# A log-sum-exp kernel: the bias of three heads added on GpSimd, most tiles loaded whole, and the last batch written in four parts

## The chip, the cores and the metric

One core of one Trainium2 chip runs the kernel. The metric is the device time of one execution in microseconds (us). The kernel before took 341.03 us, the median of 11 runs (340.31 to 341.71). The profile shows one execution that took 341.08 us by the same clock; its span, from the first to the last instruction, is 339.1 us.

## The reference

```python
B, S, D, H = 8, 2048, 2048, 8            # x: (B, S, D) f32, bias: (H, D // H) f32
x_heads = x.reshape(B, S, H, Dh).transpose(0, 2, 1, 3) + bias[None, :, None, :]
x_tiled = np.repeat(x_heads, 2, axis=2)  # every row twice
mx = x_tiled.max(axis=-1, keepdims=True)
lse = mx.squeeze(-1) + np.log(np.exp(x_tiled - mx).sum(axis=-1))   # (B, H, 2 S)
```

For each batch, row and head, 256 values get that head's bias; the logarithm of the sum of their exponentials is written twice side by side. The input has 134.2 MB, the output 1.05 MB.

## The kernel before

**Tiles.** A tile `xt` holds 256 rows of one batch: 128 partitions with K = 2 rows of 2048 numbers, 2 MB. There are 64 tiles, 8 to a batch, and NBUF = 9 buffers for them. The kernel takes no maximum; it sums exp(x + bias), and the eight heads are split by how the bias comes in.

**Heads 0 and 1 (NPE = 2).** `add_bias` (L139 to L151) makes x + bias in PSUM on TensorE. For each of the two rows k it first writes the bias with a small bf16 matmul (L145), then adds x by a matmul with the identity (L150; each f32 matmul appears as two instructions). ScalarE takes the exponential in PSUM and sums it in the same instruction (`sum_biased`, L156), whose sum is fetched by a following read of the accumulator.

**Heads 2 to 7.** ScalarE replaces x by exp(x) in the tile (`exp_inplace`, L164), for a whole tile in one instruction of 3072 numbers a partition. VectorE multiplies each head's 256 values by exp(bias), held in `w_rep` in SBUF, and sums them (`weigh`, L170): 12 instructions a tile, each with a read of the accumulator.

**Results.** Sums of a batch are collected in `R[b]` (of the last batch only the first seven tiles; the last tile has `Rz`). `finish` (L181) transposes them on TensorE (L186), takes the logarithm and doubles it on ScalarE (L199) and stores it (L214). A full batch is finished two tiles after its end, with one transfer of 64 rows of 2 KB. The last batch is finished in three parts: the seven tiles (eight transfers of 7 rows, one a head) after the first piece of the last tile's second row, and the two rows of the last tile at the very end, one transfer each, all on SyncE's queue.

**Order.** The order of each engine's instructions is that of the program (`manual_schedule`). SyncE issues all loads. `load(t + 9)` (L248) stands after the work of tile t, since it reuses that tile's buffer. A transfer on SyncE's queue also waits for the one eight transfers earlier: eight semaphores are used in turn, which the trace shows in the semaphores that the issues name. `pieces` (L68) sets how a tile is loaded and worked on: tiles 0 to 54 whole; 55 to 59 in two rows of 1 MB; 60 to 62 in four halves of 512 KB; the last tile, 63, in seven pieces (`LAST_CUTS`, L22), down to 128 KB.

GpSimd works only at the start: it splits the bias in three bf16 parts (L116 to L120) and moves them with three small transfers of its own (L122).

Of the kernel before, what the change touches and what calls it, by code (L numbers as in the profile page):

```python
# [9 lines left out]
F32 = mybir.dt.float32  # L10
BF16 = mybir.dt.bfloat16
ACT = mybir.ActivationFunctionType
ALU = mybir.AluOpType


K = 2


NPE = 2
NBUF = 9  # L20

LAST_CUTS = [[0, 1024, 2048], [0, 512, 1024, 1536, 1792, 2048]]  # L22
# [3 lines left out]
def kernel(  # L26
# [6 lines left out]
    nc = tc.nc  # L33
    P = nc.NUM_PARTITIONS
    B, S, D = x.shape
    H, Dh = bias.shape
    assert D == H * Dh and S % (P * K) == 0
    NBLK = S // (P * K)
    T = B * NBLK
    CPE = NPE * Dh  # L40
    CW = D - CPE
    MM = 512
    assert CPE <= MM

    sb = ctx.enter_context(tc.tile_pool(name="sb", bufs=1))
    pp = ctx.enter_context(
        tc.tile_pool(name="pp", bufs=1, space=bass.MemoryType.PSUM)
    )

    brow = sb.tile([1, D], F32, name="brow")  # L50
    w_rep = sb.tile([P, CW], F32, name="w_rep")
    ident = sb.tile([P, P], F32, name="ident")
    ones = sb.tile([1, P], F32, name="ones")
    ones3 = sb.tile([3, P], BF16, name="ones3")
# [1 line left out]
    bparts = sb.tile([1, 3, CPE], BF16, name="bparts")  # L56
    brest = sb.tile([1, 2, CPE], F32, name="brest")

    nblk = [NBLK] * (B - 1) + [NBLK - 1]
    R = [sb.tile([P, K, H, nblk[b]], F32, name=f"R{b}") for b in range(B)]  # L60
    Rz = sb.tile([P, K, H], F32, name="Rz")
    junk = [sb.tile([P, Dh], F32, name=f"junk{i}") for i in range(2)]
    res = [sb.tile([H * NBLK, P, K, 2], F32, name=f"res{i}") for i in range(2)]
    xts = [sb.tile([P, K, D], F32, name=f"xt{i}") for i in range(NBUF)]
    ps = [pp.tile([P, MM], F32, name=f"ps{i}") for i in range(6)]
    tps = [pp.tile([P, K, P], F32, name=f"tps{i}") for i in range(2)]

    def pieces(t):  # L68

        left = T - 1 - t  # L70
        if left > 8:
            return [(0, K, 0, D)]
        if left > 3:
            return [(k, k + 1, 0, D) for k in range(K)]
        cuts = [[0, D // 2, D]] * K if left else LAST_CUTS
        return [
            (k, k + 1, c0, c1) for k in range(K) for c0, c1 in zip(cuts[k], cuts[k][1:])
        ]

    def rows_of(t):  # L80

        b, blk = divmod(t, NBLK)
        v = x[b, blk * P * K : (blk + 1) * P * K, :]
        if t < T - 1:
            return v.rearrange("(p k) d -> p k d", k=K)
        return v.rearrange("(k p) d -> p k d", k=K)

    def load(t):
        for k0, k1, c0, c1 in pieces(t):
            nc.sync.dma_start(  # L90
                out=xts[t % NBUF][:, k0:k1, c0:c1], in_=rows_of(t)[:, k0:k1, c0:c1]
            )
# [5 lines left out]
    for set_idx, (_name, funcs) in enumerate(get_activation_tables(nc.m.arch).items()):  # L98
        if ACT.Exp in funcs and ACT.Ln in funcs:
            nc.scalar.add_instruction(  # L100
                mybir.InstLoadActFuncSet(
                    name=nc.get_next_instruction_name(),
# [4 lines left out]
    nc.scalar.dma_start(out=brow, in_=bias.rearrange("h j -> (h j)").unsqueeze(0))  # L107
    for t in range(NBUF):
        load(t)
# [12 lines left out]
        nc.gpsimd.dma_start(out=b3[i : i + 1, :], in_=bparts[:, i])  # L122


    for i, c in enumerate(range(0, CW, MM)):
        nc.tensor.matmul(  # L126
            ps[i],
            lhsT=ones,
            rhs=brow[:, CPE + c : CPE + c + MM],
            start=True,  # L130
            stop=True,
        )
        nc.scalar.activation(out=w_rep[:, c : c + MM], in_=ps[i], func=ACT.Exp)  # L133


    n_ps = [0]
# [2 lines left out]
    def add_bias(views):  # L139

        got = []
        for v in views:
            p = ps[n_ps[0] % len(ps)]
            n_ps[0] += 1
            nc.tensor.matmul(  # L145
                p[:, 0:CPE], lhsT=ones3, rhs=b3, start=True, stop=False
            )
            got.append(p)
        for p, v in zip(got, views):
            nc.tensor.matmul(p[:, 0:CPE], lhsT=ident, rhs=v, start=False, stop=True)  # L150
        return got  # L151

    def sum_biased(p, dst):
        for h in range(NPE):
            c = h * Dh
            nc.scalar.activation(  # L156
                out=p[:, c : c + Dh],
                in_=p[:, c : c + Dh],
                func=ACT.Exp,
                accum_out=dst(h),  # L160
            )

    def exp_inplace(v):
        nc.scalar.activation(out=v, in_=v, func=ACT.Exp)  # L164

    def weigh(v, h, dst):
        c = h * Dh - CPE
        j = junk[n_junk[0] % 2]
        n_junk[0] += 1
        nc.vector.tensor_tensor_reduce(  # L170
            out=j,
            in0=v,
            in1=w_rep[:, c : c + Dh],
            scale=1.0,
            scalar=0.0,
            op0=ALU.mult,
            op1=ALU.add,
            accum_out=dst,
        )

    def finish(b, src, n_blk, k_rows, base, i, engines):  # L181

        nr = H * n_blk
        n = P * k_rows * 2
        for k in range(k_rows):
            nc.tensor.transpose(out=tps[i][0:nr, k], in_=src(k), identity=ident)  # L186
        tp = tps[i]
        rs = res[i]
        tv = bass.AP(
            tensor=tp.tensor,  # L190
            offset=tp.offset,
            ap=[[tp.ap[0][0], nr], [1, P], [P, k_rows], [0, 2]],
        )
        rv = bass.AP(
            tensor=rs.tensor,
            offset=rs.offset,
            ap=[[rs.ap[0][0], nr], [2 * k_rows, P], [2, k_rows], [1, 2]],
        )
        nc.scalar.activation(out=rv, in_=tv, func=ACT.Ln)  # L199

        parts = [(0, H)] if n_blk * n in (n, 2 * S) else [(h, h + 1) for h in range(H)]
        for q, (h0, h1) in enumerate(parts):
            rows = (h1 - h0) * n_blk
            ov = bass.AP(
                tensor=out.tensor,
                offset=out.offset + (b * H + h0) * 2 * S + 2 * base,
                ap=[[n if n_blk > 1 else 2 * S, rows], [1, n]],
            )
            iv = bass.AP(
                tensor=rs.tensor,  # L210
                offset=rs.offset + h0 * n_blk * rs.ap[0][0],
                ap=[[rs.ap[0][0], rows], [1, n]],
            )
            engines[q % len(engines)].dma_start(out=ov, in_=iv)  # L214


    for t in range(T):
        b, blk = divmod(t, NBLK)
        xt = xts[t % NBUF]
        last = t == T - 1  # L220

        def sum_at(k, h):
            return Rz[:, k, h : h + 1] if last else R[b][:, k, h, blk : blk + 1]

        for k0, k1, c0, c1 in pieces(t):
            if c0 == 0:
                got = add_bias([xt[:, k, 0:CPE] for k in range(k0, k1)])
            w0 = max(c0, CPE)
            if w0 < c1:
                exp_inplace(xt[:, k0:k1, w0:c1])  # L230
            if c0 == 0:
                for k in range(k0, k1):
                    sum_biased(got[k - k0], lambda h: sum_at(k, h))
            for k in range(k0, k1):
                for c in range(w0, c1, Dh):
                    weigh(xt[:, k, c : c + Dh], c // Dh, sum_at(k, c // Dh))
            if last and k0 == K - 1 and c0 == 0:
                finish(
                    b,
                    lambda k: R[b][:, k].rearrange("p h n -> p (h n)"),  # L240
                    NBLK - 1,
                    K,
                    0,
                    1,
                    [nc.sync],
                )
        if t + NBUF < T:
            load(t + NBUF)  # L248

        fb, at = divmod(t - 2, NBLK)  # L250
        if fb >= 0 and at == NBLK - 1:
            finish(
                fb,
                lambda k: R[fb][:, k].rearrange("p h n -> p (h n)"),
                NBLK,
                K,
                0,
                fb % 2,
                [nc.sync],
            )  # L260
    for k in range(K):
        finish(B - 1, lambda _: Rz[:, k], 1, 1, S - (K - k) * P, k, [nc.sync])

    order.__exit__(None, None, None)

# [29 lines left out]
```

The softmax here doesn't subtract the row's maximum and nothing guards it: scores larger than these inputs give would overflow.

## Time and profile before

| | |
|---|---|
| median of 11 runs | 341.03 us |
| the profiled execution, and its span | 341.08 us, 339.1 us |
| busy: ScalarE, VectorE, TensorE, GpSimd | 295.4, 271.8, 234.8, 6.3 us |
| DMA, mean over the span | 400 GB/s; 425 to 432 GB/s in the middle |
| HBM read, written | 134.23 MB, 1.05 MB |
| instructions of VectorE counted as busy | 1538 |

How to read it: rows of a page or an answer give line, engine, operation, output and inputs with their shapes, the number of instructions, their busy time and the mean of one in ns, and then the idle time just before them with what ended it. The "DMA" and "GB/s" rows cut the span into 40 equal slices of 8.48 us. The chain of waits follows the work that ended last back in time. Besides what the views print, the trace records the time of every DMA packet, and for each transfer the time at which each of the 16 DMA engines reported its share as landed; a few numbers below are read from those records and say so.

### The profile page before, as it was taken

The numbers are of one execution on the slowest core, as the hardware profiler recorded it, in microseconds if no ns is written. First come the engines' busy times: TensorE is split into PE (matmuls) and PEld (weight loads), VectorE is DVE, ScalarE is ACT, GpSimd is POOL, SyncE is SP. The second block draws the span as 40 slices with busy tenths as digits, with TensorE's granted clock in tenths as the row PEclk, the third lists the DMA queues.
The fourth block names the chain that finished last, engine by engine and source line by source line (L and its number), as shares of the span: only waits on it lengthen the run. The fifth ranks groups of instructions, "written<-read, shape, count | busy, mean of one in ns | idle before, by whom it ended". The sixth has DMA issues, their size and how long they took to land. (4 is left out here: it accounts for less than half of the span.)

```text
span 339.1 us, 3449 instructions
## 1 busy us (share of the span) xinstructions
PE 234.8 (69%) x408; PEld 67.9 (20%) x408; DVE 271.8 (80%) x1538; ACT 295.4 (87%) x609; POOL 6.3 (2%) x14
## 2 busy tenths in 40 slices
PE   6296775767785767875765775966766567887892
PEld 2032121112121111221221221321221211221220
DVE  0429999998887887897898698788798788989784
ACT  2379999998997997988998998998899899998994
POOL 6000000000000000000000000000000000000000
PEclk9999877785877785877898777598777898577655
DMA  8999999999999999999999999999999999988950
GB/s 304 429 431 426 426 431 424 431 427 426 427 426 432 425 425 429 430 427 426 431 425 425 431 429 424 430 430 425 427 426 432 430 411 420 422 349 283 308 202 17
DMA packets 12921, 135.50 MB, mean 400 GB/s; under 512 B 1625, under 2 KB 1897, under 8 KB 4577
## 3 DMA queue, kind: packets, MB, share of 16 engines
q1 hardware_dynamic: 12800, 135.27, 95.7%
q14 instruction: 20, 0.16, 0.1%
q8 instruction: 3, 0.05, 0.1%
q10 hardware_dynamic: 2, 0.01, 0.0%
q0 software_dynamic: 96, 0.00, 0.0%
HBM read 134.23 MB, written 1.05 MB: 399 GB/s over the span
## 5 line engine op out<-in xcount | busy, mean ns | idle before, releaser
L170 DVE CUSTOM_DVE_ANT_0 junk<-xt,w_rep 128x256 f32<-128x256 f32 x768 | 271.0, 420 | 63.3 <-ACT xt L164 63.0
L150 PE MATMUL ps<-xt,ident 128*128 128x512 f32 x256 | 184.0, 851 | 88.5 <-DMA xt<-in_x_dram 88.0
L164 ACT ACTIVATE xt<-xt 128x3072 f32<-128x3072 f32 (+4 forms) x83 | 179.4, 2172 | 19.3 <-DMA xt<-in_x_dram 15.0
L156 ACT ACTIVATE ps<-ps 128x256 f32<-128x256 f32 x256 | 94.6, 370 | 14.7 <-PE ps L150 9.8
L150 PEld LDWEIGHTS ps<-xt,ident 128*128 128x128 f32 x256 | 55.1, 242 | 166.6 <-DMA xt<-in_x_dram 124.6
L170 DVE DVE_READ_ACCUMULATOR2_ANT R<- 128x1 f32 x756 | 61.5, 81 | 0.0
L145 PE MATMUL ps<-b,ones 3*128 3x512 bf16 x128 | 47.2, 441 | 6.6 <-DVE R L170 6.6
L156 ACT ACTIVATION_READ_ACCUMULATOR ps<-ps 128x1 f32 x256 | 48.7, 190 | 0.0
L145 PEld LDWEIGHTS <-ones 3*128 3x128 bf16 x128 | 8.0, 96 | 82.8 <-issue 74.6
L126 PE MATMUL ps<-brow,ones 1*128 1x512 f32 x6 | 5.5, 1078 | 3.1 <-DMA brow<-in_bias_dram 3.1
L133 ACT ACTIVATE w_rep<-ps 128x512 f32<-128x512 f32 x3 | 1.8, 597 | 5.4 <-PE ps L126 5.4
L199 ACT ACTIVATE res<-tps 64x512 f32<-64x512 f32 (+2 forms) x10 | 5.3, 534 | 1.3 <-PE tps L186 1.3
L186 PEld LDWEIGHTS tps<-ident,R 128*64 128x64 f32 (+1 forms) x16 | 2.7, 171 | 9.6 <-ACT ps L156 3.6
L186 PE MATMUL tps<-ident,R 128*64 128x128 f32 (+1 forms) x16 | 4.6, 387 | 0.0
L186 PE MATMUL tps<-ident,Rz 128*8 128x128 f32 x2 | 0.8, 375 | 3.5 <-DVE Rz L170 2.8
L126 PEld LDWEIGHTS ps<-brow,ones 1*128 1x128 f32 x6 | 1.8, 324 | 5.1 <-issue 5.1
L100 ACT ACT_TABLE_LOAD x1 | 1.3, 1283 | 0.7 <-PEq L279 0.7
L122 POOL DMA_DIRECT2D b<-bparts x3 | 1.6, 540 | 0.0
L117 POOL TENSOR_TENSOR brest<-brow,bparts 1x512 f32<-1x512 f32 x1 | 1.1, 1142 | 0.1
L119 POOL TENSOR_TENSOR brest<-brest,bparts 1x512 f32<-1x512 f32 x1 | 1.1, 1142 | 0.1
L186 PEld LDWEIGHTS tps<-ident,Rz 128*8 128x8 f32 x2 | 0.2, 83 | 4.2 <-DVE Rz L170 3.1
L170 DVE DVE_READ_ACCUMULATOR2_ANT Rz<- 128x1 f32 x12 | 1.0, 82 | 0.0
(11 smaller groups left out, 3.0 us busy)
## 6 DMA issues: line engine op xcount, KB each, us to landing
xt<-in_x_dram SPq DMA_DIRECT2D x55, 2048.0 KB
xt<-in_x_dram SPq DMA_DIRECT2D x10, 1024.0 KB
xt<-in_x_dram SPq DMA_DIRECT2D x14, 512.0 KB
out_dram<-res SPq DMA_DIRECT2D x7, 128.0 KB
xt<-in_x_dram SPq DMA_DIRECT2D x3, 256.0 KB
xt<-in_x_dram SPq DMA_DIRECT2D x2, 128.0 KB
out_dram<-res SPq DMA_DIRECT2D x8, 14.0 KB
b<-bparts POOLq DMA_DIRECT2D x3, 1.0 KB, 5.8
```

What stands on the lines that cost most here:

```text
L100: nc.scalar.add_instruction(mybir.InstLoadActFuncSet(name=nc.get_next_instruction_name(), act_func_set_id=set_idx,))
L117: nc.gpsimd.tensor_sub(brest[:, 0], bp, bparts[:, 0])
L122: nc.gpsimd.dma_start(out=b3[i : i + 1, :], in_=bparts[:, i])
L126: nc.tensor.matmul(ps[i], lhsT=ones, rhs=brow[:, CPE + c : CPE + c + MM], start=True, stop=True,)
L133: nc.scalar.activation(out=w_rep[:, c : c + MM], in_=ps[i], func=ACT.Exp)
L145: nc.tensor.matmul(p[:, 0:CPE], lhsT=ones3, rhs=b3, start=True, stop=False)
L150: nc.tensor.matmul(p[:, 0:CPE], lhsT=ident, rhs=v, start=False, stop=True)
L156: nc.scalar.activation(out=p[:, c : c + Dh], in_=p[:, c : c + Dh], func=ACT.Exp, accum_out=dst(h),)
L164: nc.scalar.activation(out=v, in_=v, func=ACT.Exp)
L170: nc.vector.tensor_tensor_reduce(out=j, in0=v, in1=w_rep[:, c : c + Dh], scale=1.0, scalar=0.0, op0=ALU.mult, op1=ALU.add, accum_out=dst,)
L186: nc.tensor.transpose(out=tps[i][0:nr, k], in_=src(k), identity=ident)
L199: nc.scalar.activation(out=rv, in_=tv, func=ACT.Ln)
```

## The change

Each tile but the last two is now worked on whole. Heads 0 and 1 and the last three heads (5 to 7) are done as before. For heads 2 to 4 (NG = 3), GpSimd adds the bias to both rows of the tile in place (`g_add`, one instruction of 1536 numbers a partition), with the bias of those heads replicated in `b_rep`. One tile later, ScalarE takes the exponential of that part (`exp_inplace(g_part(t - 1))`) and VectorE sums it with one `tensor_reduce` (`g_sum`). A tile's buffer is therefore free one tile later, and the load behind it is `load(t + 8)` after tile t. `w_rep` moves from SBUF to PSUM; `ps` has four buffers for six, and both transposed outputs share one PSUM tile. The last two tiles (NLATE = 2) are done as before: tile 62 in two rows, tile 63 in the same seven pieces.

The last batch is written in four parts: its first six tiles (`R`, eight transfers of 6 rows) after the first piece of tile 63, issued by GpSimd; tile 62 (`Ry`, one transfer of 8 rows of 2 KB) after the first piece of the second row of tile 63; the first row of tile 63 before its last piece; the second row at the end; the last three on SyncE. The rows of a store are now listed in `parts`; for a full batch this is still one transfer of 64 rows.

```diff
+NG = 3
+NLATE = 2
...
-    w_rep = sb.tile([P, CW], F32, name="w_rep")
+    b_rep = sb.tile([P, NG * Dh], F32, name="b_rep")
...
-    nblk = [NBLK] * (B - 1) + [NBLK - 1]
+    nblk = [NBLK] * (B - 1) + [NBLK - 2]
+    Ry = sb.tile([P, K, H], F32, name="Ry")
...
-    ps = [pp.tile([P, MM], F32, name=f"ps{i}") for i in range(6)]
-    tps = [pp.tile([P, K, P], F32, name=f"tps{i}") for i in range(2)]
+    w_rep = pp.tile([P, CW], F32, name="w_rep")
+    ps = [pp.tile([P, MM], F32, name=f"ps{i}") for i in range(4)]
+    tpair = pp.tile([P, 2, K, P], F32, name="tpair")
+    tps = [tpair[:, i] for i in range(2)]
...
-        if left > 8:
+        if left > 1:
             return [(0, K, 0, D)]
-        if left > 3:
-            return [(k, k + 1, 0, D) for k in range(K)]
-        cuts = [[0, D // 2, D]] * K if left else LAST_CUTS
+        cuts = [[0, D]] * K if left else LAST_CUTS
...
-    for i, c in enumerate(range(0, CW, MM)):
+    for c in range(0, CW, MM):
         nc.tensor.matmul(
-            ps[i],
+            w_rep[:, c : c + MM],
...
-        nc.scalar.activation(out=w_rep[:, c : c + MM], in_=ps[i], func=ACT.Exp)
+    nc.scalar.activation(out=b_rep, in_=w_rep[:, 0 : NG * Dh], func=ACT.Copy)
+    for c in range(0, CW, MM):
+        w = w_rep[:, c : c + MM]
+        nc.scalar.activation(out=w, in_=w, func=ACT.Exp)
...
+    def g_part(t):
+        return xts[t % NBUF][:, :, CPE : CPE + NG * Dh]
+
+    def g_add(t):
+        nc.gpsimd.tensor_tensor(out=g_part(t), in0=g_part(t), in1=b_tile, op=ALU.add)
+
+    def g_sum(t):
+        b, blk = divmod(t, NBLK)
+        nc.vector.tensor_reduce(
+            out=R[b][:, :, NPE : NPE + NG, blk],
+            in_=g_part(t).rearrange("p k (h j) -> p k h j", j=Dh),
+            op=ALU.add,
+            axis=mybir.AxisListType.X,
+        )
...
+        if n_blk == 1:
+            step, parts = 2 * S, [H]
+        elif n_blk == NBLK:
+            step, parts = n, [nr]
+        else:
+            step, parts = n, [n_blk] * H
...
+        if left >= NLATE:
+
+            got = add_bias([xt[:, k, 0:CPE] for k in range(K)])
+            g_add(t)
+            w0 = CPE + NG * Dh
+            exp_inplace(xt[:, :, w0:D])
+            if t:
+                exp_inplace(g_part(t - 1))
+            for k in range(K):
+                sum_biased(got[k], lambda h: sum_at(k, h))
+            for k in range(K):
+                for c in range(w0, D, Dh):
+                    weigh(xt[:, k, c : c + Dh], c // Dh, sum_at(k, c // Dh))
+            if t:
+                g_sum(t - 1)
+        for k0, k1, c0, c1 in pieces(t) if left < NLATE else []:
+            if left == 0 and c1 == D and k0 > 0:
+
+                finish(
+                    B - 1,
+                    lambda k: Rz[:, k0 - 1],
...
-            if last and k0 == K - 1 and c0 == 0:
...
-        if t + NBUF < T:
-            load(t + NBUF)
+            if left == 0 and c0 == 0:
+                if k0 == 0:
+                    finish_batch(B - 1, nc.gpsimd)
+                elif k0 == 1:
+                    finish(B - 1, lambda k: Ry[:, k], 1, K, S - 2 * K * P, 0, nc.sync)
+        if left == NLATE:
+            exp_inplace(g_part(t))
+            g_sum(t)
+        if 0 < t and t - 1 + NBUF < T:
+            load(t - 1 + NBUF)
...
-    for k in range(K):
-        finish(B - 1, lambda _: Rz[:, k], 1, 1, S - (K - k) * P, k, [nc.sync])
+    finish(B - 1, lambda _: Rz[:, K - 1], 1, 1, S - P, 1, nc.sync)
```

## The prediction

> **What bounds the kernel now.** I read first the page (busy times, the slices, the chain), then the queue's own waits, the chain in order of time, and the groups by form for prices.
>
> ```profile
> PE 234.8 (69%) x408; PEld 67.9 (20%) x408; DVE 271.8 (80%) x1538; ACT 295.4 (87%) x609; POOL 6.3 (2%) x14
> ...
> GB/s 304 429 431 426 426 431 424 431 427 426 427 426 432 425 425 429 430 427 426 431 425 425 431 429 424 430 430 425 427 426 432 430 411 420 422 349 283 308 202 17
> ...
> q14 instruction: 20, 0.16, 0.1%
> ```
>
> No engine is full; the DMA runs flat at about 427 GB/s and falls to 280 to 350 in the last five slices. The chain, in order of time, says the same:
>
> ```profile
> 183.10 39.03 DMA xt<-in_x_dram
> ...
> 291.87 17.57 DMA xt<-in_x_dram
> ...
> 311.73 10.17 DMA xt<-in_x_dram
> ...
> 321.94 2.07 PE ps L150 x2
> ...
> 329.74 2.02 PE ps L150 x2
> ...
> 333.24 0.53 ACT xt L164
> ...
> 336.42 0.37 ACT res L199
> ```
>
> Loads until 321.9 us, then rows of tile 62 and 63 through TensorE (2.07 us a row at half clock), then ScalarE, VectorE, the transpose and the last store.
>
> Why does the rate fall? The landing records answer. Of the first load the 16 DMA engines report between 7.74 and 8.42 us, of tile 54 between 273.37 and 283.43, and at 294.27 one engine is 11.0 us behind the first, 8 behind the next slowest. That engine sets when a tile is complete. Its delay grows in steps of about 0.94 us ((11.03 - 0.68) / 11), and each step follows a packet of q14, an instruction fetch of 8 KB: the load packet behind it takes 1265 ns where others take 613. Eleven of these, before 294 us, come every 126 rows of VectorE's program (at rows 79, 205, 331 and so on; waits count as rows). So **fetching VectorE's instructions delays one of the 16 DMA engines**, and all loads wait for it. With eight transfers in flight the other 15 run ahead until the pieces shrink; then they stall, which is the fall in the slices. Their rate costs nothing; the slow engine's work does.
>
> [...]
>
> ```profile
> L170 DVE CUSTOM_DVE_ANT_0 junk<-xt,w_rep 128x256 f32<-128x256 f32 x768 | 271.0, 420 | 63.3 <-ACT xt L164 63.0
> L164 ACT ACTIVATE xt<-xt 128x3072 f32<-128x3072 f32 x55 | 151.8, 2760 | 19.3 <-DMA xt<-in_x_dram 15.0 <-DVE R L170 3.8
> L164 ACT ACTIVATE xt<-xt 128x1536 f32<-128x1536 f32 x10 | 14.7, 1474 | 0.0
> L122 POOL DMA_DIRECT2D b<-bparts x3 | 1.6, 540 | 0.0
> L117 POOL TENSOR_TENSOR brest<-brow,bparts 1x512 f32<-1x512 f32 x1 | 1.1, 1142 | 0.1
> ```
>
> **Part by part, a whole tile.** A tile's period is 4.89 us (the fast engines' 54 tiles) and about 5.0 with stores and fetches; everything that stays below it is hidden.
> - VectorE: twelve `weigh` start 0.346 us apart (timeline), 4.15 us. Now six, plus a sum of 1536. [...] 6 x 0.41 = 2.5; the sum at `weigh`'s slope (256 in 0.27) is 1.6 to 1.75. Total 4.2, hidden. Ends: 0.346 each (no loss; a gain has no reason) and 0.61 (PSUM at half rate), see rivals.
> - ScalarE: 2.67 + 1.87 = 4.54 us. Two of 1536, 1.38 apart in the timeline, cost 2.76, so 4.63, with the batch's logarithm 4.70: hidden, though with 0.3 to spare. The start (first sums at 18.2 us, unchanged, since they wait for `b3`) leaves 1.4 us more backlog, made good within some 35 tiles.
> - GpSimd: [...] it has a whole tile of slack. Ends: 1.8 us (three times the 599 ns of the one-input casts of 512 on this engine) and 5.0, where it would bind.
> - SyncE: loads go out a tile later, with six to seven tiles (over 29 us) still in flight. The slow engine never runs dry. What stands behind a waiting load on SyncE is only loads and finished batches' stores. Full batches' stores do not change. Nothing.
> - The four `ps` buffers still hold two tiles; TensorE's work is the same.
>
> **What VectorE's shorter program saves.** 24 rows a tile and 1.3 waits become 13 and one to two and a half. By tile 61 that is 870 to 950 rows: (870 - 79) / 126 = 6.3, or 6.9, so 7 fetches where there were 12. ScalarE gets one fetch more, on an engine that is only 3 us behind. Gain: 4 x 0.94 = 3.8 by 294 us and some 0.5 for the twelfth among small packets. **Larger packets:** 16 KB take 613 ns, 8 KB 312, 4 KB 159; per engine and tile 8 x 613 = 4.90, 16 x 312 = 4.99, 32 x 159 = 5.09. Five tiles save 0.09, two 0.18: 0.8 by packet times, 0.4 by landings (1.245 us a 512 KB piece). I take 0.4. Tile 61 then lands at 8.42 + 61 x 4.888 + 6 stores x 0.34 + 7 x 0.94 = 315.2, against 320.65 before; from the differences 320.65 - 4.7 = 315.9. I take **315.4**; all else follows from it (call it L).
>
> **The end: what is late next.** Loads no longer: the last piece lands at L + 10.1 = 325.5 (before 330.87). ScalarE now has, from L: tile 61, 1.38 + 1.38 (tile 60's part) + 1.87; tile 61's own part, 1.38; tile 62, two rows of 2.27 (timeline at 288 us); tile 63: 0.53 + 0.89, logarithm of R 0.5, 0.95, 0.89, logarithm of Ry 0.5, 0.53 twice, logarithm 0.3, 0.73. Sum 16.9: 332.3. GpSimd's add for tile 61, done at L + 3.5, is covered by the 4.6 before it. VectorE has two sums (1.7) and 6 + 12 + 12 `weigh`: the last sum of tile 61 ends at L + 7.8, and in order it finishes at L + 17.9 at 0.41 each. From its end to the span's end it took 339.12 - 335.95 = 3.2 us (transpose, logarithm, store). SyncE path: 315.4 + 17.9 + 3.2 = **336.5**.
>
> GpSimd's stores: the logarithm of R ends at L + 12.5 = 327.9. Eight issues of 0.54 bring the last to 331.7. Landing is the unknown. The three transfers of GpSimd in this trace took 5.8 us, but each waited twice behind 613 ns load packets; loads end at 325.5, so 4.6. [...] With 1.1 us from landing to end: 334.8 to 338.6; I take 331.7 + 4.6 + 1.1 = **337.4**. This is later than SyncE's path, so it ends the span: 339.1 - 337.4 = 1.7 saved. The profiled 341.08 stands at the median 341.03, so I predict **339.3**. The 5.2 us won in the loads shrink because ScalarE, free before the end until now, gets tile 61's extra part and the last rows all at once.
>
> **Rivals.**
> 1. TensorE takes the gain. If tile 61 finds it at half clock (as from 316.5 us on before), its rows run at 2.07 + 0.5 = 2.57 us: tile 61 until 319.7, then three rows to 327.4, transposes 1.5, the row of 63 to 331.5, where before it was 331.78. Same tail: span 338.8, 340.8 us. For: the slow rows in the chain. Against: with whole tiles the clock was full two thirds of the time.
> 2. Slower: GpSimd's stores come one by one. If each needs the 1.0 us between landings of the three small ones, and the full 5.8, the last lands at 327.9 + 7 x 1.0 + 5.8 = 340.7: span 341.8, 343.7 us. It decides from a last landing of 338.0 on (span 339.1). Against: those spacings are two load packets each.
> 3. Slower: VectorE becomes the bound. Above (5.0 - 1.75) / 6 = 0.54 us a `weigh`, each tile grows; at 0.61 it is 5.4 us, 61 x 0.4 = 24 us more, 365 us. [...] For: neither PSUM input nor overlap is in this trace. [...]
> 4. The change adds nothing to the loads, if fetches are not what delays the engine: then L stays near 320.2, and the span is about 342, 344 us.
>
> **How the numbers follow.** 0.2% (0.7 us) is about what a measurement of this kernel tells from no change. Forecast 0.62 (337.0 to 340.3); rival 1 0.14 (same); rival 2 0.10; rival 3 0.09; rival 4 0.05. Faster 0.62, same 0.14, slower 0.24. The range runs from a last store at 2 us with six fetches, which leaves SyncE's path less 1 us and VectorE at 0.346 (337.0), to 342.8, part of rival 2; left out are rival 3, most of 4, and the end of 2.
>
> **What would show it.** VectorE 856 busy instructions (2 + 62 x 13 + 2 x 24); seven of its fetches; the last engine of tile 61 about 7 us after the first; last load landed near 325.5; the slices near 427 GB/s to about 310 us; rows of `weigh` at 0.41 apart, the add at 3.4 us. Wrong, if `weigh` waits for GpSimd, if ScalarE is never idle from 60 us on, or if the loads still end near 330.

## The result, and the profile after

The changed kernel took 338.0 us, the median of 8 runs (337.75 to 338.1); the kernel before took 341.1 us in the same comparison (31 runs, 339.93 to 341.99). The ratio is 0.991, with an interval of 0.9899 to 0.9921: **0.9% faster**. The profiled execution took 338.01 us, with a span of 336.2 us, 2.9 us less than before.

These are lines of the page of the kernel after: the span, busy times, the rate of the DMA in 40 slices, the queue of instruction fetches, and two groups of transfers that GpSimd issues (last column: us from issue to landing).

```profile
span 336.2 us, 2806 instructions
...
PE 245.8 (73%) x410; PEld 71.7 (21%) x410; DVE 244.7 (73%) x856; ACT 301.4 (90%) x660; POOL 224.4 (67%) x84
...
GB/s 299 431 429 435 419 433 429 427 423 430 425 432 429 429 424 431 427 432 424 432 424 423 431 433 423 431 427 427 431 426 429 431 426 425 429 427 421 358 42 16
...
q14 instruction: 15, 0.12, 0.1%
...
out_dram<-res POOLq DMA_DIRECT2D x8, 12.0 KB, 1.7
b<-bparts POOLq DMA_DIRECT2D x3, 1.0 KB, 5.9
```

The reader sees three things. VectorE has 856 busy instructions where it had 1538, and only a tenth less busy time. The three slices before the end of the loads in which the rate fell to between 283 and 349 GB/s are gone: from the second slice it holds at 419 or more up to slice 37, which ends at 311 us. And ScalarE has gained 6 us and stands at 90% of the span.

The landing records say why the rate holds. Tile 61 was complete at 315.12 us; before, at 320.65. Its last DMA engine came 7.1 us after the first (call this the lag), where in the kernel before the lag had grown to 11.0 us by 294 us. VectorE's instruction fetches ahead of it were 7 (12 before), at its rows 70, 196, 325, 451, 577, 703 and 843. From 0.88 us of lag at the first tile (0.68 before) this is (7.11 - 0.88) / 7 = 0.89 us a fetch; the last step alone was 7.08 - 6.12 = 0.96 us.

The chain of the kernel after, in order of time (start, length, what), names loads until 319.8 us and then mostly ScalarE; the matmuls of the last rows at half clock (0.50 granted from 316.5 us on, 2.07 us a row before) are no longer in it. ScalarE's timeline shows that the loads stop deciding earlier than the chain says: from 315.21 us, 0.09 us after tile 61 landed, to 331.41 it works without a wait. What follows tile 61 until then is ScalarE's work.

```profile
285.10 32.51 DMA xt<-in_x_dram
...
317.63 2.15 DMA xt<-in_x_dram
...
319.97 2.74 ACT xt L194 x2
...
323.60 1.37 ACT xt L194
...
327.76 0.95 ACT xt L194
...
330.62 0.42 DVE junk L200
...
332.86 0.39 PE tpair L216
...
333.28 0.37 ACT res L229
```

The groups by form of the kernel after give the prices of the moved work:

```profile
L182 POOL TENSOR_TENSOR xt<-xt,b_rep 128x1536 f32<-128x1536 f32 x62 | 214.0, 3452 | 96.0 <-DMA xt<-in_x_dram 95.5 <-ACT b_rep L139 0.5
L194 ACT ACTIVATE xt<-xt 128x1536 f32<-128x1536 f32 x126 | 179.9, 1474 | 13.6 <-DMA xt<-in_x_dram 12.3
L200 DVE CUSTOM_DVE_ANT_0 junk<-xt,w_rep 128x256 f32<-128x256 f32 x396 | 140.5, 417 | 86.5 <-ACT xt L194 86.5
L186 DVE TENSOR_REDUCE R<-xt 128x6 f32<-128x1536 f32 x62 | 108.5, 1750 | 0.8 <-ACT xt L194 0.8
```

GpSimd's idle time (96.0 us) and ScalarE's idle time ahead of L194 (13.6 us) end mostly with a load: neither of them is what the tiles wait for. VectorE is idle behind ScalarE alone. A `weigh` of 417 ns is about as long as before (420).

### The profile page after: what moved, and what is told of

It is laid out like the page before. It is cut to its first block, busy times and chain, and to the rows that moved or that the text cites. A ratio compares the mean times of both kernels' runs of the same rounds, so it can differ in the third digit from the quotient of the medians.

```text
span 336.2 us, 2806 instructions
## 1 busy us (share of the span) xinstructions
PE 245.8 (73%) x410; PEld 71.7 (21%) x410; DVE 244.7 (73%) x856; ACT 301.4 (90%) x660; POOL 224.4 (67%) x84
## 4 chain that ended last, share of the span: by engine, by line
DMA 62%; ACT 22%; DVE 6%; PE 3%; issue 1%; SPq 0%; ACTq 0%; DVEq 0%
DMA xt<-in_x_dram 62%; ACT xt L194 15%; ACT ps L165 7%; DVE junk L200 4%; DVE R L186 2%; PE ps L159 2%; PE ps L154 1%; ACT res L229 1%; PE tpair L216 0%; DVE R L200 0%; DVE Rz L200 0%; SPq L95 0%; ACTq L194 0%; DVEq L356 0%
## 5 line engine op out<-in xcount | busy, mean ns | idle before, releaser
L182 POOL TENSOR_TENSOR xt<-xt,b_rep 128x1536 f32<-128x1536 f32 x62 | 214.0, 3452 | 96.0 <-DMA xt<-in_x_dram 95.5
L159 PE MATMUL ps<-xt,ident 128*128 128x512 f32 x256 | 191.3, 888 | 62.8 <-DMA xt<-in_x_dram 62.3
L200 DVE CUSTOM_DVE_ANT_0 junk<-xt,w_rep 128x256 f32<-128x256 f32 x396 | 140.5, 417 | 86.5 <-ACT xt L194 86.5
L194 ACT ACTIVATE xt<-xt 128x1536 f32<-128x1536 f32 (+1 forms) x132 | 183.4, 1435 | 13.6 <-DMA xt<-in_x_dram 12.3
L186 DVE TENSOR_REDUCE R<-xt 128x6 f32<-128x1536 f32 x62 | 108.5, 1750 | 0.8 <-ACT xt L194 0.8
L159 PEld LDWEIGHTS ps<-xt,ident 128*128 128x128 f32 x256 | 59.5, 257 | 155.5 <-DMA xt<-in_x_dram 102.3
L200 DVE DVE_READ_ACCUMULATOR2_ANT R<- 128x1 f32 x372 | 30.8, 83 | 0.0
L250 POOL DMA_DIRECT2D out_dram<-res x8 | 4.0, 506 | 9.3 <-ACT res L229 9.3
L132 PE MATMUL w_rep<-brow,ones 1*128 1x512 f32 x6 | 5.5, 1078 | 2.8 <-DMA brow<-in_bias_dram 2.8
L229 ACT ACTIVATE res<-tpair 64x512 f32<-64x512 f32 (+3 forms) x11 | 5.9, 540 | 1.2 <-PE tpair L216 0.9
## 6 DMA issues: line engine op xcount, KB each, us to landing
xt<-in_x_dram SPq DMA_DIRECT2D x3, 256.0 KB, 16.9
```

What stands on the lines that cost most here:

```text
L132: nc.tensor.matmul(w_rep[:, c : c + MM], lhsT=ones, rhs=brow[:, CPE + c : CPE + c + MM], start=True, stop=True,)
L182: nc.gpsimd.tensor_tensor(out=g_part(t), in0=g_part(t), in1=b_tile, op=ALU.add)
L186: nc.vector.tensor_reduce(out=R[b][:, :, NPE : NPE + NG, blk], in_=g_part(t).rearrange("p k (h j) -> p k h j", j=Dh), op=ALU.add, axis=myb ...
L200: nc.vector.tensor_tensor_reduce(out=j, in0=v, in1=w_rep[:, c : c + Dh], scale=1.0, scalar=0.0, op0=ALU.mult, op1=ALU.add, accum_out=dst,)
L250: engine.dma_start(out=ov, in_=iv)
```

## The experiments

The theory: a tile is complete when its slowest DMA engine is done, that engine carries the fetches of VectorE's instructions, and the change wins because VectorE has fewer instruction rows. What is won at the loads is given back in part at the end. Its rivals: VectorE's shorter busy time, or the whole tiles, win it. Each ratio is to the kernel before, run beside it on the same chip: 340.91 us for the first four kernels, 341.55 for the next four, 340.72 for the last two.

### Rows without work, on VectorE

```diff
+    fill = sb.tile([P, 16], F32, name="fill")
...
             if t:
                 g_sum(t - 1)
+            for i in range(11):
+                nc.vector.memset(fill[:, i : i + 1], 0.0)
```

> The changed kernel with eleven one-column memsets a tile added at the end of VectorE's work, so that VectorE's program has again some 25 rows a tile, as before the change. Theory (fetching VectorE's instructions delays one DMA engine): about 12 fetches instead of 7 before 310 us, that engine some 11 us behind instead of 7, tile 61 complete near 319.5 us instead of 315.1, and about 4.4 us more, 342 us in all. Rival (the gain is that of loading whole tiles): 338.0, as the changed kernel.

Measured: 342.83 us (342.58 to 342.97), ratio 1.0057 (1.0044 to 1.007). Two lines of its page:

```profile
PE 239.3 (70%) x410; PEld 69.4 (20%) x410; DVE 253.4 (74%) x1538; ACT 301.3 (88%) x660; POOL 224.2 (66%) x84
...
q14 instruction: 21, 0.17, 0.1%
```

The group of its fills by form (busy us, mean ns of one), and the eleven of one tile in VectorE's timeline (start, length, what):

```profile
L293 DVE MEMSET fill<- 128x1 f32 x682 | 11.9, 59 | 0.4
...
150.92 0.20 DVE L293 MEMSET fill<- 128x1 f32 x11
```

VectorE has as many busy instructions as before the change, 1538, and 12 fetches ahead of tile 61 again. Tile 61 was complete at 319.82 us with a lag of 11.97. Against the kernel after this is 4.7 us for 5 fetches, 0.94 us each, and the time rose by 4.8. A fill takes 59 ns, but the fills overlap: the eleven of a tile take 0.20 us together, 11.9 us in all.

### The same VectorE time in one row

```diff
+    fill = sb.tile([P, 704], F32, name="fill")
...
+            nc.vector.memset(fill, 0.0)
```

> The control of the run before: one memset of 704 columns a tile instead of eleven small ones, about the same 0.7 us of VectorE's time in one row. Theory: 7 or 8 fetches, tile 61 near 315.1 to 316, 338.0 to 338.8 us. Rival (VectorE's time, and not its rows, is what cost the kernel before): as slow as the eleven, 340 us or more.

Measured: 338.0 us (337.77 to 338.21), ratio 0.9916 (0.9902 to 0.9929). Two lines of its page:

```profile
PE 237.1 (70%) x410; PEld 69.2 (21%) x410; DVE 284.5 (85%) x918; ACT 301.1 (89%) x660; POOL 224.4 (67%) x84
...
q14 instruction: 16, 0.13, 0.1%
```

Its fill by form:

```profile
L292 DVE MEMSET fill<- 128x704 f32 x62 | 40.0, 645 | 5.8
```

The time is not the same, as was meant: one fill of 645 ns holds VectorE three times as long as the eleven do (40.0 us in all against 11.9), since those overlap. That makes the control stricter. VectorE is at 284.5 us, 13 us above the kernel before the change, and the time is that of the kernel after; tile 61 at 315.31 with 7 fetches. So **it is rows that cost, not time**: of these two kernels the one with more VectorE time and fewer rows is 4.8 us faster.

### The same rows on GpSimd

```diff
+    fill = sb.tile([P, 16], F32, name="fill")
...
+            for i in range(11):
+                nc.gpsimd.memset(fill[:, i : i + 1], 0.0)
```

> The changed kernel with eleven one-column memsets a tile added on GpSimd, some 1 us a tile beside its add of 3.45. Theory, with each engine's instructions fetched by a DMA engine of its own: GpSimd's six to seven fetches put another DMA engine behind by at most what VectorE's already is, 338.0 to 338.6 us. Rival (all fetches delay the same DMA engine): some 5 us later, 343 us.

Measured: 338.1 us (338.05 to 338.27), ratio 0.992 (0.9906 to 0.9933). A line of its page:

```profile
q14 instruction: 20, 0.16, 0.1%
```

Its fills by form:

```profile
L282 POOL MEMSET fill<- 128x1 f32 x682 | 26.5, 96 | 0.0
```

There are five fetches more than in the kernel after, and nothing is lost. By the landing records of tile 61 the slowest DMA engine is as it was (315.00). Behind it two others are now late, 5.0 and 3.8 us after the first, where the kernel after has one at 4.1 and the next at 2.1. So GpSimd's fetches fall on another DMA engine than VectorE's, and that one has room. They also cost it less: the load packet behind a GpSimd fetch took 0.92 to 1.14 us, behind a VectorE fetch 1.27. What counts here is the latest DMA engine, not the number of fetches in all.

### The last loads cut as before, the work whole

```diff
+    def cuts_of(t):
+        left = T - 1 - t
+        if left > 8 or left < 1:
+            return pieces(t)
+        if left > 3:
+            return [(k, k + 1, 0, D) for k in range(K)]
+        return [(k, k + 1, c, c + D // 2) for k in range(K) for c in (0, D // 2)]
...
-        for k0, k1, c0, c1 in pieces(t):
+        for k0, k1, c0, c1 in cuts_of(t):
```

> The changed kernel with only the loads of tiles 55 to 62 cut as before the change (55 to 59 in two rows, 60 to 62 in four halves); the work on the tiles is unchanged. Theory: the rate of the slices falls again near the end, as before, but only the packets' own cost is paid: tile 61 0.4 us later, 338.3 us. Rival (the fall of the rate was the loss): 3 us or more, 341 us.

Measured: 338.12 us (337.99 to 338.27), ratio 0.992 (0.9906 to 0.9933). From its page:

```profile
GB/s 299 425 434 430 425 432 427 427 427 429 425 431 425 429 429 425 432 429 424 426 428 423 434 432 425 430 427 419 436 422 434 430 416 420 424 412 402 359 86 16
DMA packets 13076, 135.46 MB, mean 403 GB/s; under 512 B 1785, under 2 KB 2057, under 8 KB 4737
```

Tile 61 was complete at 315.77 us, 0.65 later than in the kernel after, and the last piece landed at 325.91, 0.8 later; the span is 0.3 longer, and the time rose by 0.1, which the intervals don't separate from nothing. The expected fall to 280 GB/s doesn't come back with the pieces. It needs small pieces and a large lag: the kernel before has both (11 us of lag), this one has the pieces with 7 us, and the next experiment has 12 us without the pieces; neither shows it.

### Whole tiles alone, in the kernel before

```diff
-        if left > 8:
+        if left > 1:
             return [(0, K, 0, D)]
-        if left > 3:
-            return [(k, k + 1, 0, D) for k in range(K)]
-        cuts = [[0, D // 2, D]] * K if left else LAST_CUTS
+        cuts = [[0, D]] * K if left else LAST_CUTS
```

> The kernel before with only the change of its pieces: tiles 55 to 61 loaded and worked on whole, tile 62 in two rows. Theory: VectorE's program keeps its 24 rows a tile, so tile 61 is complete only 0.4 us earlier, near 320.2 us, and ScalarE and VectorE have the last tiles' work later at once: 341 us, between 340.3 and 342. Rival (loading whole is the gain): 338 us.

Measured: 341.32 us (341.12 to 341.97), ratio 1.0 (0.9992 to 1.0009). From its page:

```profile
PE 241.2 (71%) x408; PEld 69.3 (20%) x408; DVE 271.4 (80%) x1538; ACT 294.8 (87%) x596; POOL 6.3 (2%) x14
...
GB/s 300 433 429 428 426 431 426 431 422 429 433 424 426 431 427 420 435 429 428 431 423 423 431 433 424 426 432 429 429 425 427 432 427 422 430 431 409 216 52 17
```

This removes the fall of the slices at once (431 and 409 GB/s in slices 36 and 37, where the kernel before had 349 and 283), and no gain is resolved: the fast DMA engines are done sooner, but tile 61 is complete at 320.20 us, only 0.45 sooner than in the kernel before, with 12 fetches, and even that doesn't reach the end (span 339.4). **The most visible mark in the slices was not the loss.**

### The early part of the last batch on SyncE

```diff
-                    finish_batch(B - 1, nc.gpsimd)
+                    finish_batch(B - 1, nc.sync)
```

> The changed kernel with the eight stores of the last batch's first six tiles issued by SyncE instead of GpSimd. Theory: SyncE is idle then; eight issues of 0.34 us from 327.8 us on end near 330.5, 0.4 us after the logarithm of tile 62 at 330.1 and well before the last store: 338.0, within 0.3. Rival (the way through GpSimd clears the end): 1 to 3 us slower.

Measured: 338.32 us (338.15 to 338.59), ratio 0.9908 (0.9894 to 0.9922), span 336.6. Beside the kernel after (0.991, span 336.2) no difference is resolved: the choice of queue wins or costs nothing that these runs show.

### The weights in SBUF

```diff
-    w_rep = pp.tile([P, CW], F32, name="w_rep")
+    w_ps = pp.tile([P, CW], F32, name="w_ps")
+    w_rep = sb.tile([P, CW], F32, name="w_rep")
```

The matmul of the bias goes to `w_ps`; ScalarE writes its exponential to `w_rep` and copies `b_rep` from `w_ps`. Nothing else is changed.

> The changed kernel with w_rep kept in SBUF, as before the change, so that weigh has two inputs in SBUF while GpSimd adds. Theory [...]: VectorE's 3.7 us a tile and GpSimd's 3.45 no longer lie side by side, 7.2 us a tile against 4.95, up to 140 us more; at least 20 us more if only a part waits. Rival (no contention): 338.0 us, weigh 0.34 us apart.

Measured: 450.46 us (448.66 to 453.98), ratio 1.3196 (1.3138 to 1.3253). The group of `weigh` by form:

```profile
L202 DVE CUSTOM_DVE_ANT_0 junk<-xt,w_rep 128x256 f32<-128x256 f32 x396 | 327.4, 884 | 17.7 <-ACT xt L196 17.7
```

VectorE and GpSimd in one tile of its timeline (start, length, what):

```profile
203.36 0.41 DVE L202 CUSTOM_DVE_ANT_0 junk<-xt,w_rep 128x256 f32<-128x256 f32 x1
...
203.54 3.52 POOL L184 TENSOR_TENSOR xt<-xt,b_rep 128x1536 f32<-128x1536 f32 x1 [4.49 <-DVE R L202]
...
203.70 3.64 DVE L202 CUSTOM_DVE_ANT_0 junk<-xt,w_rep 128x256 f32<-128x256 f32 x1
...
207.28 0.41 DVE L202 CUSTOM_DVE_ANT_0 junk<-xt,w_rep 128x256 f32<-128x256 f32 x1
```

A `weigh` that starts once GpSimd's add runs takes 3.64 us, until just after the add's end at 207.06; those ahead and behind take 0.41. Tiles come 6.97 us apart. In the kernel after, where one of the two inputs is in PSUM, 347 of the `weigh` lie beside an add, and none takes over 0.42 us. What holds the `weigh` back is not shown, but the two kernels differ only in where `w_rep` lies. So moving `w_rep` is what makes the overlap possible, and rival 3 of the prediction was near: one buffer in another memory, 112 us (450.46 for 338.0).

### A fourth head on GpSimd

```diff
-NG = 3
+NG = 4
```

> The changed kernel with four heads through GpSimd instead of three. Theory: VectorE's program has 10 to 11 rows a tile, 5 fetches instead of 7, tile 61 1.9 us earlier; GpSimd's add takes 4.6 us, still under the 4.95 of a tile; ScalarE's tail has 0.4 us more: 336.5 us. Rival (GpSimd becomes the bound at 4.6 us, since its add is late for tile 61's part at the end or never catches up): 338 us or more.

Measured: 336.72 us (336.66 to 336.77), ratio 0.9859 (0.9844 to 0.9874), span 335.0. From its page:

```profile
q14 instruction: 14, 0.11, 0.1%
```

Its groups by form for the add and the sum:

```profile
L182 POOL TENSOR_TENSOR xt<-xt,b_rep 128x2048 f32<-128x2048 f32 x62 | 280.9, 4532 | 28.0 <-DMA xt<-in_x_dram 22.1 <-DVE R L186 4.1 <-DVE R L200 1.1
...
L186 DVE TENSOR_REDUCE R<-xt 128x8 f32<-128x2048 f32 x62 | 141.9, 2289 | 22.5 <-ACT xt L194 22.5
```

VectorE has 608 busy instructions and 5 fetches ahead of tile 61, which is complete at 313.46 us (lag 5.5): 1.7 sooner than in the kernel after, for 2 fetches fewer. The span is 1.3 us shorter; by the ratios the gain is 1.7, and their intervals don't tell the two apart. GpSimd's add now takes 4.53 us of a tile's 4.9, and a head more costs 1.08 (4.53 less the 3.45 for three). So a fifth would take about 5.6, an estimate from these two (4.53 + 1.08), and not fit.

### The part on GpSimd ends two tiles sooner

```diff
-NLATE = 2
+NLATE = 4
```

Heads 2 to 4 of tiles 60 and 61 go back to VectorE, and no part of these tiles is left over for the next one. They are still loaded and worked on whole.

> The changed kernel with NLATE = 4: tiles 60 and 61 are loaded whole but worked on as before the change, so that GpSimd's last part is tile 59's and ScalarE has nothing of an earlier tile left when tile 61 lands. Theory (what the earlier loads win is given back by ScalarE's work from tile 61 on, 6.0 us for that tile): tile 61 takes ScalarE 4.5 us, the end comes 1.4 us earlier, 336.6 us, with the same 7 fetches. Rival (the end is set by the landing of the last pieces, or by the last stores): 338.0.

Measured: 336.44 us (336.36 to 336.86), ratio 0.9871 (0.9851 to 0.9891), span 334.6. ScalarE in the timeline of the kernel after:

```profile
315.21 2.86 ACT L194 ACTIVATE xt<-xt 128x1536 f32<-128x1536 f32 x2 [0.29 <-DMA xt<-in_x_dram]
...
319.86 2.85 ACT L194 ACTIVATE xt<-xt 128x1536 f32<-128x1536 f32 x2
...
323.50 1.48 ACT L194 ACTIVATE xt<-xt 128x1536 f32<-128x1536 f32 x1
```

ScalarE in the timeline of this kernel:

```profile
315.11 2.76 ACT L194 ACTIVATE xt<-xt 128x3072 f32<-128x3072 f32 x1 [0.33 <-DMA xt<-in_x_dram]
...
319.56 1.47 ACT L194 ACTIVATE xt<-xt 128x1536 f32<-128x1536 f32 x1
...
321.83 1.47 ACT L194 ACTIVATE xt<-xt 128x1536 f32<-128x1536 f32 x1
```

In the kernel after, the pair at 315.21 is tile 61's part and the one carried over from tile 60; the pair at 319.86 is tile 61's own carried part and then the first row of tile 62, which so starts at about 321.2. Here that row starts at 319.56, and the second row at 321.83 for 323.50: 1.7 us sooner. Tile 61 was complete at the same time (315.03), so this 1.7 is work at the end alone; the last logarithm starts at 331.60 for 333.28, and the span is 1.7 shorter (334.55 for 336.23).

### Both

```diff
-NG = 3
-NLATE = 2
+NG = 4
+NLATE = 4
```

> Four heads through GpSimd (NG = 4) and NLATE = 4 together. Theory: both gains add, five fetches and the shorter end: 338.0 - 1.3 - 1.4 = 335.3 us, or a little less, since ScalarE's part left over for tile 61 was larger with four heads. Rival (one hides the other): 336.6.

Measured: 335.65 us (335.49 to 335.71), ratio 0.9843 (0.9824 to 0.9863), span 333.9: the fastest of these kernels. The gains don't quite add up: by the times it is 2.35 us, where the two alone have 1.28 and 1.56. Tile 61 is complete at 313.36, 1.7 ahead of the one with NLATE = 4 alone, but ScalarE takes it up only at 314.50 for 315.11, since it is busy until then with the larger part carried over from tile 59 and with tile 60. These 0.6 us are what reaches the end (the last logarithm at 330.96 for 331.60; span 0.7 shorter).

## Why the prediction was right, and where its size was off

The direction and the mechanism were right; the time was forecast 1.3 us too late. Step by step:

| step | forecast | measured |
|---|---|---|
| VectorE's fetches ahead of tile 61 | 7 | 7 |
| cost of a fetch | 0.94 us | 0.89 us on the mean; 0.94 between the kernel with added rows and the one after |
| tile 61 complete (L) | 315.4 | 315.12 |
| larger packets' part of that | 0.4 us | 0.45 us (whole tiles alone), 0.65 (loads cut as before) |
| last piece landed | 325.5 | 325.15 |
| `weigh` from PSUM, start to start | 0.41 us | 0.343 us (0.346 before, from SBUF) |
| the sum of 1536; GpSimd's add | 1.6 to 1.75; 3.4 us | 1.75; 3.45 us |
| ScalarE's tile, when it never waits | 4.63 us | 4.53 us |
| ScalarE's last exponential | L + 16.9 | L + 17.2 |
| VectorE's end; from there to the span's end | L + 17.9; 3.2 us | L + 17.7; 3.4 us |
| span by SyncE's path | 336.5 | 336.2 |
| landing of GpSimd's late stores | 4.6 us | 1.7 us |
| span by GpSimd's stores | 337.4 | not the end: landed at 333.26 |

The 0.41 us was the author's estimate; the trace before shows no VectorE instruction with an input from PSUM. The 3.4 us for the add is near three times the 1142 ns that L117 took for 512 numbers (3.43). The prediction's slope of 0.27 us for 256 numbers holds for the sums: 1750 ns for 1536, and 2289 for 2048 with a fourth head on GpSimd, so 539 for 512. All `weigh` have one size, so theirs is not shown.

**The step that failed** is the landing of GpSimd's late stores. The prediction took 4.6 us, from three transfers at the start that ran beside full loads, and so had these stores end the span. They landed after 1.7 us, below the 2 us at the low end of its range, which was the author's estimate, shown by no trace before. The timeline of GpSimd in the kernel after:

```profile
315.26 3.46 POOL L182 TENSOR_TENSOR xt<-xt,b_rep 128x1536 f32<-128x1536 f32 x1 [1.47 <-DMA xt<-in_x_dram]
328.05 3.98 POOL L250 DMA_DIRECT2D out_dram<-res  x8 [9.33 <-ACT res L229]
```

The eight issues start at 328.05 us, 0.50 apart, close to the forecast (327.9, 0.54). The loads had ended at 325.15, so no load packet stood ahead of these; the three transfers at the start took 5.9 us again in the same execution. With the last store landed at 333.3, 1.7 us ahead of SyncE's last (335.0), the path that the prediction had worked out beside it took over: 337.4 - 336.2 = 1.2 of the 1.3 us. The prediction named a reason, that the slow transfers each waited behind load packets, and had placed the last load at 325.5, ahead of these stores, but took off only 1.2 us for it. That the loads are the whole difference is not shown: the transfers at the start also differ in kind, from SBUF to SBUF, where these go to `out_dram`.

That the other path came within 0.3 us is in part luck: tile 61 came 0.3 us sooner than forecast, and ScalarE took 0.3 us longer after it. Three readings of the trace in the prediction are off and change nothing: of the last five slices only three show the fall (the last two are the end of the loads), the lag at 294.27 us is 10.97 us and not 11.03, and ScalarE's tile without waits took 4.44 us before, not 4.54.

**The gain that does not arrive** was right in kind. Tile 61 is complete 5.5 us sooner, the span ends 2.9 us sooner. From tile 61 to the span's end it took 18.5 us before (339.1 - 320.65), 21.1 in the kernel after, and 21.0 in the one with added rows, where tile 61 is as late as before the change. So this 2.6 us comes with the rest of the change, whatever the loads do, and it accounts for the 1.7 us by which that kernel's span is longer than the one before (340.8 for 339.1): 2.5 us more at the end (21.0 - 18.5), 0.8 less in the loads. The run with NLATE = 4 recovers 1.6: the part carried over a tile. For the other 1.0 the run with whole tiles alone gives a hint. In the kernel before, tile 61 was worked on in four pieces as they landed; with whole tiles it took 19.2 us from its landing to the span's end (339.4 - 320.2), 0.7 more than 18.5. That leaves 0.3 us open.

**The rivals.** Rival 1 (TensorE takes the gain) did not decide: three rows did run at half clock (0.50 granted until 321.4 us), 3.8 us for tile 61's two and 2.1 for the next, but the last three, at full clock, took 1.1 us each, and ScalarE never waited for them. Rival 2 (GpSimd's stores one by one, 1.0 us apart and 5.8 to land) is out at 0.50 and 1.7. Rival 3 did not come, but the kernel with the weights in SBUF shows that it would have without the move to PSUM, at nearly five times its price of 24 us. That the move would prevent it was the author's expectation, which no trace of the kernel before showed. The price that the prediction put on an input from PSUM (0.41 us a `weigh` for 0.346, and 0.61 at the far end) was not seen: 0.343 us from start to start beside 0.346. Rival 4 (fetches delay nothing) is out by the first two experiments: 4.8 us.

Left open: why a load packet behind a VectorE fetch takes twice as long (1.27 us for 0.61) is not shown, only that it does. A kernel without any VectorE fetch during the loads wasn't tried.

## What to carry to other kernels

Where loads set the time, compare when each DMA engine lands its share: here one engine, 11.0 us behind the first, set when a tile was complete, and the mean rate hid it. Count an engine's instruction rows as DMA traffic: here five more fetches of VectorE's, 0.94 us each, made the kernel 4.8 us slower, and one fill of 645 ns a tile in place of eleven of 59 won that back, with 31 us more busy time (284.5 for 253.4). Then ask what the end inherits: work postponed by a tile was free in the middle and cost 1.6 us behind the last loads, so try to stop postponing before the end.

## What the runs showed that was not expected

- A transfer that GpSimd issued landed in 1.7 us with the loads ended (SBUF to `out_dram`) and in 5.9 us beside them (SBUF to SBUF), in the same execution.
- GpSimd's instruction fetches delay another DMA engine than VectorE's, and by less a fetch (the load packet behind one took 0.92 to 1.14 us, behind one of VectorE's 1.27): with five more of them one more engine came late (5.0 us behind the first), and that cost nothing.
- Eleven fills of one column overlap on VectorE: 59 ns each, 0.20 us together.
- `weigh` with one input in PSUM costs no more than with both in SBUF (0.343 and 0.346 us); with both in SBUF beside a GpSimd add, one of them takes 3.64 us, until just after the end of the add (3.52 us).
